# The two output projections of a two-layer encoder, computed as seven products of sums of blocks instead of eight products of blocks

## The chip, the cores and the metric

The kernel runs on one core of a Trainium2 chip. The metric is the device time of one execution in microseconds (us). All inputs and outputs are float32, and the weights, tables and activations lie in DRAM at the start.

## The reference, cut to what matters

```python
def reference(x, mem, ...):                 # x: (1, 1024, 1024), mem: (1, 256, 1024)
    memn = rmsnorm(mem, mem_norm_gain)
    for l in range(2):
        h = rmsnorm(x, norm_gain[l])
        ...
        if l == 0:   # 8 global heads, 8 window heads of 64; 4 memory heads of 128
            ya, yb, ym = global_gqa(...), window_gqa(...), memory_attn(...)
            y = jnp.concatenate([ya, yb, ym], axis=-1) * jax.nn.silu(gate)
            x = x + y @ w_out_even[e]       # (1024 x 1536) @ (1536 x 1024)
        else:        # 16 neighbourhood heads of 64; 4 memory heads of 128
            yc, ym = neighborhood_attn(...), memory_attn(...)
            y = jnp.concatenate([yc, ym], axis=-1) * jax.nn.silu(gate)
            x = x + y @ w_out_odd[o]        # (1024 x 1536) @ (1536 x 1024)
    return rmsnorm(x, final_norm_gain)
```

The change concerns the two lines with `w_out`, the output projections. Each maps 1536 rows of gated attention outputs (12 tiles of 128 rows) to 1024 columns (8 tiles of 128), for 1024 tokens (two halves of 512).

## The kernel before, in words

**Layout.** Activations lie transposed: 128 features on the partitions, tokens along the free dimension. A float32 matmul is done as three matmuls in the format F32R: each operand is split into a high part (a rounded copy, `copy`, L88 on ACT) and a low part (operand minus high part), and TensorE adds high×high, high×low and low×high in PSUM. One such matmul has 512 tokens as its moving side.

**What stands ahead of an output projection.** In layer 0 the heads come in the order global pairs 0 to 3, memory heads, window pairs 0 to 3; in layer 1 the memory heads come first and then eight neighbourhood pairs. Behind each pair or memory head, `gated` (L308) projects the gate with SiLU (`gate`, L295), multiplies the head's output by it (L314 or L320), and stores the product in a DRAM tile `yd[k]`, one of 12. In layer 0 the product is stored as it is; in layer 1 it is split here, and high and low parts are stored (ACT L88, DVE L322). A window pair goes in chunks: scores (L476, L477), sums with bias on DVE (L479), exponentials on ACT, scaling with the softmax denominators on POOL (L500), transposes (L96), a split of the transposed probabilities (`p_parts`, ACT L88 and DVE L332) and the product with the values (L515). A neighbourhood pair has the same steps at L875/L876, L883, L887, L889, L96, L88/L332 and L858.

**The output projection** (`out_project`, L917). For each half of the tokens it goes over the 8 column tiles two at a time, and for these over the 12 row tiles in units of four, the unit of the memory heads first (order 2, 0, 1). For the first half and the first four column tiles that unit's matmuls are issued ahead of the others, and can stand between the matmuls of the last attention pair. `project` (L123) loads the weights of each unit and column tile (128 x 512, `wload`), splits them (`wparts`, L112: high part on POOL L118; low part L119 on DVE in layer 0 and on POOL in layer 1), and issues 12 matmuls of 512 tokens (L134). So one layer has 8 x 12 x 3 x 2 = 576 matmuls; in layer 1 the last column tile of the second half goes in two quarters of 256 tokens (L985). `y_parts` (L900) loads the gated outputs back from DRAM; in layer 0 it splits them there (ACT L88, DVE L92), through a buffer `ph`. The sink of a column tile adds the residual to the PSUM result (L940, DVE), squares it (L941, ACT) and adds the squares up (L951, POOL). `done` then makes the norm: `rstd_cols` (L204, tiny matmuls), `rows_of` (transposes, L96) and, for layer 0, `norm_split` (L217 to L219), or, behind layer 1, the scaling by norm and gain (L1100 on POOL, L1102 on DVE) and the stores of the output (L1103).

**What sets the order.** The order of the instructions of each engine is fixed when the kernel is built: a scheduler orders them by a simulated timeline and by priorities (`ahead`, with the table `AHEAD`, L29). Each engine runs its instructions in that order, and SP issues nearly all the transfers, in one queue. PSUM has 8 banks of 512 columns. SBUF tiles come from pools by tag; a new tile with a tag waits until the oldest one of that tag has been read for the last time. Tag `H` has 16 tiles, which hold the normed input of a layer (8 tiles, high and low).

## Time and profile before

| what | us |
|---|---|
| three timed runs | 1612.15, 1610.36, 1612.3 (median 1612.15) |
| the profiled execution, its own time | 1608.82 |
| the span of its trace | 1607.0 |

The profiled execution's own time and the span of its trace differ by 1.82 us, which lie before the first and after the last traced instruction. Its mean granted TensorE clock is 0.989 of full speed.

How to read the profile: PE is TensorE (matmuls), PEld its loads of stationary operands, DVE is VectorE, ACT ScalarE, POOL GpSimd, SP the queue that issues transfers. A group of instructions is told as its line, engine and operation, output<-inputs by the program's names, shapes, count, busy time and mean duration in ns, then the idle time of the engine just before them and what ended most of it. A row of a timeline is start, length, engine, line, operation, tiles, count, and in brackets the wait ahead of it and what ended that wait. A row of the view of windows gives for a stretch its length, then for each engine its busy time and its number of instructions, the granted clock of TensorE, the share of the DMA engines' time in use, and GB/s. The chain of waits goes back from the last instruction, at each step to what released it.

In the profiled execution, layer 0's output projection lies between about 680 us (where its first matmuls stand between those of the last window pair) and 849 us, and layer 1's between about 1441 us and 1595 us, near the end of the span.

### The profile page before, as it was taken

The numbers are of one execution on the slowest core, as the hardware profiler recorded it, in microseconds if no ns is written. First come the engines' busy times: TensorE is split into PE (matmuls) and PEld (weight loads), VectorE is DVE, ScalarE is ACT, GpSimd is POOL, SyncE is SP. The second block draws the span as 40 slices with busy tenths as digits, with TensorE's granted clock in tenths as the row PEclk, the third lists the DMA queues.
The fourth block names the chain that finished last, engine by engine and source line by source line (L and its number), as shares of the span: only waits on it lengthen the run. The fifth ranks groups of instructions, "written<-read, shape, count | busy, mean of one in ns | idle before, by whom it ended". The sixth has DMA issues, their size and how long they took to land.

```text
span 1607.0 us, 24242 instructions
## 1 busy us (share of the span) xinstructions
PE 1551.9 (97%) x8394; PEld 1323.8 (82%) x8394; DVE 957.5 (60%) x2124; ACT 706.6 (44%) x1626; POOL 655.3 (41%) x801
## 2 busy tenths in 40 slices
PE   6999999999999999989999999999999999999997
PEld 6899888888887888867788888888888888888886
DVE  7768577766667678864764444655555555554122
ACT  8633564655446355641313333534544445443110
POOL 2522232332323133224454335544444444445885
PEclk7999999999999999999999999999999999999998
DMA  9524111025211111135552324213222222235772
GB/s 352 180 97 152 66 40 53 29 50 83 75 66 27 67 62 50 50 117 185 182 171 87 104 87 125 83 66 91 64 76 83 66 79 79 71 107 177 238 260 79
DMA packets 97858, 167.88 MB, mean 104 GB/s; under 512 B 9504, under 2 KB 30240, under 8 KB 97736
## 3 DMA queue, kind: packets, MB, share of 16 engines
q1 hardware_dynamic: 96760, 165.51, 32.4%
q8 instruction: 66, 1.08, 0.3%
q10 hardware_dynamic: 976, 0.82, 0.2%
q14 instruction: 56, 0.46, 0.1%
HBM read 120.17 MB, written 36.70 MB: 98 GB/s over the span
## 4 chain that ended last, share of the span: by engine, by line
PE 85%; DVE 7%; ACT 3%; DMA 3%; issue 2%; POOL 0%; SPq 0%; DVEq 0%; ACTq 0%; POOLq 0%
PE pj L163 42%; PE sa L134 8%; PE tr L96 7%; PE pj L134 5%; PE s L134 3%; PE pv L816 3%; PE pj L617 2%; PE pv L858 2%; DVE pl L332 2%; PE s L875 1%; PE s L876 1%; PE sa L787 1%; PE pv L515 1%; PE sa L788 1%; DVE st L792 1%
## 5 line engine op out<-in xcount | busy, mean ns | idle before, releaser
L163 PE MATMUL pj<-H,wh 128*128 128x512 f32 x1952 | 628.3, 397 | 1.7 <-ACT bt L941 1.5
L163 PEld LDWEIGHTS pj<-H,wh 128*128 128x128 f32 x1952 | 358.8, 188 | 71.4 <-POOL wh L118 1.9
L163 PE MATMUL pj<-H,wl 128*128 128x512 f32 x976 | 386.3, 396 | 0.0
L118 POOL TENSOR_SCALAR wh<-wraw 128x512 fp32r<-128x512 f32 x226 | 151.4, 672 | 396.4 <-PE pj L163 252.0
L88 ACT ACTIVATE ph<-tr 128x512 fp32r<-128x512 f32 (+2 forms) x336 | 177.9, 540 | 243.9 <-PE tr L96 232.4
L332 DVE TENSOR_TENSOR pl<-tr,ph 128x512 fp32r<-128x512 f32 (+2 forms) x336 | 205.0, 615 | 101.9 <-ACT ph L88 98.9
L163 PEld LDWEIGHTS pj<-H,wl 128*128 128x128 f32 x976 | 183.6, 188 | 37.4
L119 POOL TENSOR_TENSOR wl<-wraw,wh 128x512 fp32r<-128x512 f32 x136 | 180.0, 1329 | 23.3 <-ACT wh L88 13.4
L795 POOL TENSOR_SCALAR P<-P,st 128x1024 f32<-128x1024 f32 x64 | 76.0, 1188 | 171.7 <-DVE st L794 162.0
L119 DVE TENSOR_TENSOR wl<-wraw,wh 128x512 fp32r<-128x512 f32 x116 | 90.3, 789 | 63.4 <-POOL wh L118 61.7
L96 PE MATMUL tr<-ident,P 128*128 128x128 f32 x816 | 123.0, 273 | 2.4 <-DVE pl L332 2.2
L889 POOL TENSOR_SCALAR pn<-pn,st 128x384 f32<-128x384 f32 (+1 forms) x128 | 71.6, 567 | 100.3 <-DVE st L888 99.4
L96 PEld LDWEIGHTS tr<-ident,P 128*128 128x128 f32 x816 | 95.7, 140 | 14.0 <-PE sa L788 7.1
L887 ACT ACTIVATE pn<-pn,st 128x384 f32<-128x384 f32 (+1 forms) x128 | 74.4, 583 | 47.3 <-DVE st L886 46.6
L792 DVE TENSOR_REDUCE st<-sa 128x1 f32<-128x1024 f32 x64 | 77.6, 1217 | 15.8 <-PE sa L788 13.5
L793 ACT ACTIVATE P<-sa,st 128x1024 f32<-128x1024 f32 x64 | 71.5, 1117 | 32.3 <-PE tr L96 14.5
L883 DVE CUSTOM_DVE_ANT_0 pn<-s,bm 128x384 f32<-128x384 f32 x96 | 51.4, 554 | 43.5 <-PE s L876 39.9
L816 PE MATMUL pv<-pl,va 128*128 128x256 f32 x256 | 69.5, 297 | 6.3 <-DVE pl L332 6.1
L617 PE MATMUL pj<-ah,H 128*128 128x256 f32 x384 | 73.1, 286 | 0.0
L235 DVE TENSOR_TENSOR vt<-pj,rows 128x512 f32<-128x512 f32 x60 | 41.2, 686 | 53.4 <-PE pj L163 53.4
L88 ACT ACTIVATE bt<-pv 64x512 f32<-64x512 f32 (+1 forms) x80 | 40.8, 510 | 71.8 <-PE pv L816 25.9
L816 PE MATMUL pv<-ph,va 128*128 128x256 f32 x256 | 72.1, 298 | 0.0
(323 smaller groups left out, 3142.6 us busy)
## 6 DMA issues: line engine op xcount, KB each, us to landing
wraw<-w_o SPq DMA_DIRECT2D x80, 256.0 KB, 2.6
wraw<-w_oe SPq DMA_DIRECT2D x48, 256.0 KB, 3.0
wraw<-w_oo SPq DMA_DIRECT2D x48, 256.0 KB, 3.1
wraw<-w_e SPq DMA_DIRECT2D x44, 256.0 KB, 2.5
k<-k SPq DMA_DIRECT2D x36, 256.0 KB, 3.7
wraw<-w_mem SPq DMA_DIRECT2D x32, 256.0 KB, 4.3
y<-yb SPq DMA_DIRECT2D x12, 512.0 KB, 2.7
y<-sg SPq DMA_DIRECT2D x24, 256.0 KB, 2.4
```

What stands on the lines that cost most here:

```text
L88: return self.nc.scalar.activation(out, in_, AF.Copy, scale=scale)
L96: self.nc.tensor.transpose(o, i, self.ident)
L118: nc.gpsimd.tensor_scalar(hf, raw, 1.0, 1.0, op0=OP.mult, op1=OP.mult)
L119: (nc.gpsimd if self.wsplit[1] == "pool" else nc.vector).tensor_tensor(lf, raw, hf, op=OP.subtract)
L134: self.last = nc.tensor.matmul(a[:, :n], s[:, k, :], moving(u * UNIT + k, c, n)[m], start=(u == units[0] and k == 0 and i == 0), stop=(u = ...
L163: last = nc.tensor.matmul(a[:, :n], s[:, kt % UNIT, :], m, start=(kt == 0 and i == 0), stop=(kt == KT - 1 and i == 2))
L332: nc.vector.tensor_tensor(pl[:, :n], tr[:, :n], ph[:, :n], op=OP.subtract)
L617: self.last = nc.tensor.matmul(a[:, b * 256:(b + 1) * 256], x[kt][:, t], w, start=(kt + b + i == 0), stop=(kt == KT - 1 and i == 2), skip_ ...
L792: nc.vector.tensor_reduce(st[:, 0:1], s, axis=AX.X, op=OP.max, negate=True)
L795: nc.gpsimd.tensor_scalar(pt, pt, st[:, 2:3], 0.5, op0=OP.mult, op1=OP.mult)
L816: nc.tensor.matmul(o[:, :256], v[:, c + k, kv, :], part[:, k * 256:(k + 1) * 256], start=(c + k == 0 and part is parts[0]), stop=(c + k == ...
L887: nc.scalar.activation(o, o, AF.Exp, bias=st[:, 1:2], accum_out=st[:, 2:3])
```

## The change

The 8 column tiles, the 12 row tiles and the 1024 tokens are each halved. With the weights as four blocks (a11 and a12: columns 0 to 3 with the first and the second half of the rows; a21 and a22: columns 4 to 7 with the same) Winograd's form of Strassen's scheme computes the four result blocks from seven products. The row tiles are renumbered by `ROWS`, in the weights too (on the host, as part of the layout): the first half holds the memory heads 0 to 3 and the pairs 0 and 1, the second half the pairs 2 to 7. In the program's order the products are

1. a11 x y(first half of rows, second tokens), to banks x, and to the result c11 (columns 0 to 3, second tokens)
2. s1 = a21 + a22, x t1 = y(first rows, first tokens) - y(first rows, second tokens), to banks y, and to c22 (columns 4 to 7, first tokens)
3. s2 = s1 - a11, x t2 = y22 - t1, added to banks x; to c12 (columns 0 to 3, first tokens). Here y22 is the second rows' first tokens
4. s3 = a11 - a21, x t3 = y22 - y(first rows, first tokens), added to banks x; to c22 and c21 (columns 4 to 7, second tokens)
5. s4 = a12 - s2, x y22, added to banks y; to c12. The first token half is done, and its norm runs beside product 6
6. a12 x y21 (second rows, second tokens), to banks x; c11 is done
7. a22 x t4 = t2 - y21, its result subtracted from c21

Each product has 4 column tiles x 6 row tiles x 3 = 72 matmuls of 512 tokens: 504 a layer instead of 576. The last column tile of product 7 in layer 1 goes in two quarters of 256 tokens, of 18 matmuls each instead of 36. A weight unit is now 128 x 384 (three row tiles, 9 matmuls), and 56 of them come up per layer instead of 48 of 128 x 512. Their high part is copied on ACT; their low part (L962) is taken on DVE, or for a11, a12 and a22 on DVE and POOL by turns (`either`). The blocks a11 and s1 are kept in tiles of tag `H`.

`gated` now stores, for the six heads or pairs of the first half, four pieces of 512 tokens: high and low part of the second tokens, the difference first minus second tokens (a subtraction on POOL), and the first tokens; for the other six it stores the product as it is, in both layers.

```diff
+ROWS = (8, 9, 10, 11, 0, 1, 2, 3, 4, 5, 6, 7)
...
-    def gated(self, w, nt, y, dst, parts=False):
+    def gated(self, w, nt, y, dst):
...
+        with self.ahead("gate"):
+            nc.vector.tensor_tensor(y, y, sg, op=OP.mult)
+            if len(dst.shape) == 2:
                 nc.sync.dma_start(dst, y)
+                return
+            nc.gpsimd.tensor_tensor(sg[:, first], y[:, first], y[:, second], op=OP.subtract)
+            h, l = sg.bitcast(F32R)[:, second], y.bitcast(F32R)[:, second]
+            self.copy(h, y[:, second])
+            nc.vector.tensor_tensor(l, y[:, second], h, op=OP.subtract)
+            for i, t in enumerate((sg[:, second], y[:, second], sg[:, first], y[:, first])):
+                nc.sync.dma_start(dst[:, i, :], t)
...
+    def y_parts(self, yd, tags, kind, t=None, y22=None):
...
+                if kind == "y11":
+                    load(tile.bitcast(F32), y0[:, 0:2, :])
+                    continue
+                if kind == "t1":
+                    load(t[k], y0[:, 2, :])
+                    raw = t[k]
+                elif kind == "t2":
+                    load(y22[k], y1[:, first])
+                    minus(t[k], y22[k], t[k])
+                    raw = t[k]
...
+                self.copy(hi, raw)
+                (nc.gpsimd if kind == "t1" else nc.vector).tensor_tensor(lo, raw, hi, op=OP.subtract)
...
+    def w_parts(self, raw, engine):
+        h, l = (self.st(t, [128, UNIT, 128], F32R, pool=self.base, bufs=4)[:, :3] for t in ("wh", "wl"))
...
+        self.copy(hf, raw)
+        engine.tensor_tensor(lf, raw, hf, op=OP.subtract)
...
     def out_project(...):
...
+                    elif kind == "s1":
+                        raw = ws[i][:, c]
+                        nc.gpsimd.tensor_tensor(raw, raw, load(a(4 + i, 0)[:, c]), op=OP.add)
+                    elif kind == "s2":
+                        raw = ws[i][:, c]
+                        nc.vector.tensor_tensor(raw, raw, wa[i][:, c], op=OP.subtract)
...
+                    yield self.w_parts(raw, self.either() if kind[0] == "a" else nc.vector)
...
+        def residual(x, nt, half):
+            nc.sync.dma_start(x, res[nt][:, 512 * (2 - half):512 * (3 - half)])
+        def plus(x, p, op=OP.add):
+            nc.vector.tensor_tensor(x, x, p, op=op)
...
+        for i in range(4):
+            product(y, xb[i], weights(i, "s2"), False)
+            residual(at(c12, i), i, 2)
+            with self.ahead("sink"):
+                plus(at(c12, i), xb[i])
```

In the changed file the lines are six or more further on: L500 is there L506, L515 is L521, L889 is L895, and L134's matmuls stand at L1018.

**What moves.** The first place is POOL at the last window pair of layer 0. P tiles are the probabilities of a chunk of that pair (L500 and L506 scale them), wh and wl a weight unit's high and low part, mk, sg, q and k in the changed kernel tiles of t1 and its parts, and H a tile of s1. Before:

```order
L500 TENSOR_SCALAR P_7586<-P_7586,st_7583 128x384 x2
L500 TENSOR_SCALAR P_7594<-P_7594,st_7583 128x384 x2
L118 TENSOR_SCALAR wh_7978<-wraw_7976 128x512
L500 TENSOR_SCALAR P_7660<-P_7660,st_7657 128x384 x2
L500 TENSOR_SCALAR P_7668<-P_7668,st_7657 128x384 x2
L500 TENSOR_SCALAR P_7734<-P_7734,st_7731 128x384 x2
L500 TENSOR_SCALAR P_7742<-P_7742,st_7731 128x256 x2
L118 TENSOR_SCALAR wh_8008<-wraw_8006 128x512
L118 TENSOR_SCALAR wh_8014<-wraw_8012 128x512
L118 TENSOR_SCALAR wh_8044<-wraw_8042 128x512
```

In the changed kernel:

```order
L506 TENSOR_SCALAR P_7696<-P_7696,st_7693 128x384 x2
L506 TENSOR_SCALAR P_7704<-P_7704,st_7693 128x384 x2
L931 TENSOR_TENSOR mk_8056<-H_8226,mk_8056 128x512
L962 TENSOR_TENSOR wl_8012<-H_7996,wh_8011 128x384
L955 TENSOR_TENSOR q_8060<-mk_8056,q_8060 128x512
L1003 TENSOR_TENSOR H_8154<-H_8154,wraw_8156 128x384
L955 TENSOR_TENSOR k_8061<-sg_8057,k_8061 128x512
L1003 TENSOR_TENSOR H_8154<-H_8154,wraw_8172 128x384
L955 TENSOR_TENSOR k_8062<-sg_8057,k_8062 128x512
L1003 TENSOR_TENSOR H_8190<-H_8190,wraw_8192 128x384
L1003 TENSOR_TENSOR H_8190<-H_8190,wraw_8208 128x384
L931 TENSOR_TENSOR mk_8056<-H_8226,mk_8056 128x512
```

There the scaling of the pair's last chunk (P_7770; before it is P_7734) comes behind these rows and the next two:

```order
L962 TENSOR_TENSOR wl_8042<-H_8026,wh_8041 128x384
L931 TENSOR_TENSOR sg_8057<-H_8227,sg_8057 128x512
L506 TENSOR_SCALAR P_7770<-P_7770,st_7767 128x384 x2
L506 TENSOR_SCALAR P_7778<-P_7778,st_7767 128x256 x2
L931 TENSOR_TENSOR sg_8057<-H_8227,sg_8057 128x512
```

Before, POOL's scalings of the last two chunks follow one upon the other with no other work between them; in the changed kernel twelve subtractions and additions of the output projection stand between P_7704 and P_7770.

The second place is PE at the end of the same pair (`pv` is its product with the values, `tr` a transpose or, in the changed kernel, also a bank of banks x or y). Before:

```order
L515 MATMUL pv_7732<-pl_7781,v_5851 128x2x128
L515 MATMUL pv_7732<-ph_7780,v_5851 128x2x128
L515 MATMUL pv_7732<-pl_7781,v_5851 128x2x128
L515 MATMUL pv_7732<-ph_7791,v_5851 128x2x128
L515 MATMUL pv_7732<-pl_7792,v_5851 128x2x128
L134 MATMUL sa_7932<-k_7892,wh_8008 128x512 x2
L134 MATMUL sa_7932<-k_7892,wl_8009 128x512
```

In the changed kernel:

```order
L521 MATMUL pv_7768<-ph_7803,v_5881 128x2x128
L521 MATMUL pv_7768<-pl_7804,v_5881 128x2x128
L521 MATMUL pv_7768<-ph_7816,v_5881 128x2x128
L1018 MATMUL tr_7925<-q_7911,wh_8028 128x512 x2
L1018 MATMUL tr_7925<-q_7911,wl_8029 128x512
L1018 MATMUL tr_7925<-q_7912,wh_8028 128x512 x2
L1018 MATMUL tr_7925<-q_7912,wl_8029 128x512
L1018 MATMUL tr_7925<-k_7913,wh_8028 128x512 x2
```

Before, the values of the last chunk are followed by matmuls on the rows of unit 0; in the changed kernel the last column tile of product 1 stands inside them, and its other three column tiles (54 matmuls) stand ahead of the last chunk's transposes.

The third place is POOL at the last neighbourhood pair of layer 1 (`pn` are the probabilities of a block of 128 queries). Before:

```order
L889 TENSOR_SCALAR pn_15230<-pn_15230,st_15231 128x256
L119 TENSOR_TENSOR wl_15575<-wraw_15572,wh_15574 128x512
L889 TENSOR_SCALAR pn_15240<-pn_15240,st_15241 128x384
L889 TENSOR_SCALAR pn_15259<-pn_15259,st_15260 128x384
L889 TENSOR_SCALAR pn_15279<-pn_15279,st_15280 128x384
L889 TENSOR_SCALAR pn_15299<-pn_15299,st_15300 128x384
L889 TENSOR_SCALAR pn_15321<-pn_15321,st_15322 128x384
L889 TENSOR_SCALAR pn_15346<-pn_15346,st_15347 128x384
L118 TENSOR_SCALAR wh_15604<-wraw_15602 128x512
```

In the changed kernel:

```order
L895 TENSOR_SCALAR pn_15229<-pn_15229,st_15230 128x256
L955 TENSOR_TENSOR k_15640<-H_15636,k_15640 128x512
L962 TENSOR_TENSOR wl_15591<-H_15575,wh_15590 128x384
L955 TENSOR_TENSOR q_15642<-H_15637,q_15642 128x512
L1003 TENSOR_TENSOR H_15662<-H_15662,wraw_15664 128x384
L1003 TENSOR_TENSOR H_15662<-H_15662,wraw_15680 128x384
L1003 TENSOR_TENSOR H_15698<-H_15698,wraw_15700 128x384
L1003 TENSOR_TENSOR H_15698<-H_15698,wraw_15716 128x384
L895 TENSOR_SCALAR pn_15263<-pn_15263,st_15264 128x256
L895 TENSOR_SCALAR pn_15273<-pn_15273,st_15274 128x384
L931 TENSOR_TENSOR H_15637<-mk_15807,H_15637 128x512
L962 TENSOR_TENSOR wl_15621<-H_15605,wh_15620 128x384
```

Before, the scalings of the last blocks stand with few weight splits (L118, L119) between them; in the changed kernel the parts of t1 and the sums s1 stand in groups of up to six between two scalings.

300 lines of the change are left out of this document (185 added, 115 removed).

## The prediction

> **What bounds the kernel now.** I read the page first, then the chain of waits, then windows around the two projections, then the timelines of single engines there.
>
> On the page, the first rows are the span and the busy times, and the row of shares is the chain that ended last, by engine:
>
> ```profile
> span 1607.0 us, 24242 instructions
> PE 1551.9 (97%) x8394; PEld 1323.8 (82%) x8394; DVE 957.5 (60%) x2124; ACT 706.6 (44%) x1626; POOL 655.3 (41%) x801
> PE 85%; DVE 7%; ACT 3%; DMA 3%; issue 2%; POOL 0%; SPq 0%; DVEq 0%; ACTq 0%; POOLq 0%
> ```
>
> TensorE is the bound: busy for 97% of the span. Whatever takes matmuls away gains their full time, as long as nothing else becomes late. The chain in order of time has, in the two projections, these pieces (start, length, what):
>
> ```profile
> 713.28 3.25 DMA ph<-y
> ...
> 1481.29 4.73 DMA mk<-y
> ...
> 1544.00 16.48 PE s L134 x72
> 1560.48 16.48 PE pj L134 x72
> ```
>
> The last two give the price of a matmul of 512 tokens: 16.48/72 = 0.2289 us from start to start. The first two are transfers of gated outputs back from DRAM, that TensorE waits for. The windows show how much it waits:
>
> ```profile
> core 0: us, PE busy (x) PEld busy (x) DVE busy (x) ACT busy (x) POOL busy (x), PEclk, DMA share, GB/s
> 680.00:849.00 169.00, 158.67 (x725) 128.20 (x724) 102.10 (x169) 48.46 (x96) 71.70 (x80) 0.99 0.50 159
> 688.00:709.00 21.00, 19.22 (x111) 16.19 (x110) 13.42 (x35) 9.56 (x27) 7.43 (x13) 1.00 0.20 64
> 709.00:725.00 16.00, 10.15 (x43) 7.22 (x40) 8.23 (x15) 6.29 (x11) 0.00 (x0) 0.89 0.66 213
> 725.00:849.00 124.00, 121.29 (x530) 97.86 (x531) 74.41 (x103) 27.63 (x45) 61.07 (x62) 1.00 0.55 176
> 1441.00:1481.00 40.00, 40.00 (x218) 34.60 (x217) 20.21 (x70) 16.85 (x44) 20.96 (x27) 1.00 0.46 150
> 1481.00:1486.00 5.00, 3.42 (x16) 2.28 (x14) 1.38 (x2) 1.10 (x2) 3.61 (x4) 1.00 0.82 233
> 1540.00:1560.00 20.00, 20.00 (x89) 16.43 (x88) 5.27 (x8) 1.90 (x3) 19.92 (x24) 1.00 0.69 225
> ```
>
> In layer 0's projection (680 to 849) TensorE is idle for 169.00 - 158.67 = 10.3 us: 1.8 in 688 to 709, beside the last window pair's chain, 5.9 in 709 to 725, where that pair's output goes to DRAM and back, and 2.7 behind it. In layer 1's it is idle for 5.00 - 3.42 = 1.6 us, and full in 1441 to 1481. Between 709 and 725 the granted clock is 0.89, and the timeline of TensorE shows why:
>
> ```profile
> 717.39 1.43 PE L134 MATMUL sa<-k,wh 128*128 128x512 f32 x2 [3.24 <-ACT k L88]
> 718.61 0.63 PE L134 MATMUL sa<-k,wl 128*128 128x512 f32 x1
> ...
> 721.12 0.40 PE L134 MATMUL sa<-k,wl 128*128 128x512 f32 x1
> ```
>
> Behind the wait, eight matmuls start between 717.39 and 721.12: 3.73 us instead of 8 x 0.2289 = 1.83. A long wait costs 1.9 us more behind it.
>
> **Matmuls that go.** 576 - 504 = 72 per layer, 144 in all, and all stand on the path: 144 x 0.2289 = **-33.0 us**.
>
> **Stalls that go.** Products 1 and 2 need the first six row tiles alone, whose heads are long done; the last pairs are first asked for in product 3, 144 matmuls or 33.0 us into the projection, and the round trip through DRAM took less than the 16 us of its window. So 10.3 + 1.9 (layer 0) and 1.6 (layer 1) go: **-13.8 us**. (The 2.7 behind 725 I count with it, since the order of that part is replaced as a whole.) If the first two products were delayed by something else, part of this cover would go as well; that is the next part.
>
> **What is added on DVE and POOL.** Per layer DVE gets 68 subtractions of two SBUF operands at 128x384 (weights: 44 low parts, 24 sums) and 30 at 128x512 (parts of t1 to y21), besides 32 sums with PSUM in place of 16; POOL gets 20 of 128x384 and 36 of 128x512 (18 differences, 6 low parts, 12 sums of squares), and no more copies of weights. The prices, in the timelines of POOL and DVE:
>
> ```profile
> 743.70 0.91 POOL L118 TENSOR_SCALAR wh<-wraw 128x512 fp32r<-128x512 f32 x1 [0.31 <-PE sa L134]
> 781.42 1.53 POOL L951 TENSOR_TENSOR vt<-vt,bt 128x512 f32<-128x512 f32 x1 [3.89 <-ACT bt L941]
> 842.24 2.54 POOL L119 TENSOR_TENSOR wl<-wraw,wh 128x512 fp32r<-128x512 f32 x2
> 1596.35 1.41 POOL L1100 TENSOR_TENSOR sg<-sg,vt 128x256 f32<-128x256 f32 x2 [8.13 <-ACT vt L88]
> ```
>
> ```profile
> 743.43 0.69 DVE L119 TENSOR_TENSOR wl<-wraw,wh 128x512 fp32r<-128x512 f32 x1 [2.81 <-POOL wh L118]
> 744.04 1.28 DVE L940 TENSOR_TENSOR yb<-sa,pl 128x512 f32<-128x512 f32 x2
> 745.24 0.68 DVE L119 TENSOR_TENSOR wl<-wraw,wh 128x512 fp32r<-128x512 f32 x1
> 781.72 1.78 DVE L119 TENSOR_TENSOR wl<-wraw,wh 128x512 fp32r<-128x512 f32 x1
> 1594.87 0.42 DVE L940 TENSOR_TENSOR yb<-pj,pl 128x256 f32<-128x256 f32 x1
> ```
>
> POOL: 2.54/2 = 1.27 for 512 columns, 1.41/2 = 0.70 for 256, so 0.98 for 384. DVE: 743.43 to 745.24 holds three of 512 columns, 0.60 each; 0.42 for 256, so 0.50 for 384. Beside each other they are dearer: at 781.72 DVE's subtraction took 1.78 in place of 0.69 and ended at 783.50, 0.55 behind POOL's end at 782.95; POOL's copy at 743.70, beside a subtraction of DVE, took 0.91. DVE's sums at 744.04, whose one operand is in PSUM, ran beside that same copy at their usual length. So subtractions of SBUF operands take turns with POOL. Their sum per layer is 68 x 0.50 + 30 x 0.60 = 52 us on DVE and 20 x 0.98 + 36 x 1.27 = 65 us on POOL, 117 us together, against 504 x 0.2289 = 115.4 us of matmuls. Neither engine is over its time alone; in strict turns the two just fill the projection, so each piece that comes late is late by a turn, and the order's slack (units of weights ahead, four buffers) is what hides it. POOL was busy for 19.92 us of 20.00 in 1540 to 1560, with 5.27 on DVE beside it and TensorE full, so such a load can be carried. I price lateness in layer 0 at 4 us (0 to 8), in layer 1 at 2 (0 to 4).
>
> The Trainium skill, "SBUF — State Buffer", section "SBUF: two separate sides", says that the pair of ports which the two engines share is "an exclusive lock, not a bandwidth split", held for a whole instruction by whichever of a DVE operation with two SBUF inputs and a GpSimd operation started first. The rows above agree (1.78 in place of 0.69). Without such a lock the 4 and the 2 would fall away, and the sum would be 6 us lower.
>
> **New waits at the start of layer 0's projection.** In the timelines of POOL (first row), TensorE and DVE, in the chain, in the page's groups and in its transfers stand the prices of what follows the last gate projection:
>
> ```profile
> 696.81 4.32 POOL L500 TENSOR_SCALAR P<-P,st 128x384 f32<-128x384 f32 x8 [8.50 <-DVE st L495]
> ```
>
> ```profile
> 687.12 0.39 PE L163 MATMUL pj<-H,wl 128*128 128x512 f32 x1
> ```
>
> ```profile
> 715.75 1.23 DVE L314 TENSOR_TENSOR yb<-yb,sg 128x1024 f32<-128x1024 f32 x1
> ```
>
> ```profile
> 630.23 0.59 PE pv L515 x5
> 631.53 0.44 PE tr L96 x4
> ```
>
> ```profile
> L88 ACT ACTIVATE ph<-tr 128x512 fp32r<-128x512 f32 (+2 forms) x336 | 177.9, 540 | 243.9 <-PE tr L96 232.4
> ...
> wraw<-w_oe SPq DMA_DIRECT2D x48, 256.0 KB, 3.0
> ```
>
> The last window pair's last two chunks were scaled one behind the other, in the eight operations of the first row. By the order, twelve operations of POOL now stand between the two chunks: six of 512 and six of 384 columns, 6 x 1.27 + 6 x 0.98 = 13.5 us. The first chunk's four are through at 696.81 + 4 x 4.32/8 = 699.0, so the last one's first two are done at 699.0 + 13.5 + 1.1 = 713.6 without turns lost to DVE, and at 717.6 if DVE takes 8 turns of 0.50; I take 716. TensorE has, from 688 (the last gate projection's last matmul starts at 687.12), 54 matmuls of product 1 (12.4 us) and of the pair 30 values at 0.59/5 = 0.118, 24 transposes at 0.44/4 = 0.11 and 8 scores of 384 columns, by their width 0.17 each: 7.5 us. It stands at 707.9, so it waits **8.1 us** (5.7 to 9.7), and 1.9 more at half speed behind it. Then product 2's last two row tiles lie in a tile of tag `sg` that comes free only with the gating of this pair: copy 0.54, subtraction 0.7, gating 1.23, transfer 3.0, the new tile's high part 0.54 and two operations on POOL 2.54, with 0.6 for the issues 9.2 us behind the last values, in which TensorE has 33 matmuls, 7.6 us: **1.6 us** (0 to 4). With 4 for turns, layer 0 gets 8.1 + 1.9 + 1.6 + 4 = **+15.6 us**.
>
> **New waits in layer 1's projection.** The first matmuls of the projection used to follow the last gate projection's at once, as the timeline of TensorE, the chain and the page's group of scalings show:
>
> ```profile
> 1444.19 0.39 PE L163 MATMUL pj<-H,wl 128*128 128x512 f32 x1
> ```
>
> ```profile
> 1441.83 1.85 PE pj L163 x8
> ```
>
> ```profile
> L889 POOL TENSOR_SCALAR pn<-pn,st 128x384 f32<-128x384 f32 (+1 forms) x128 | 71.6, 567 | 100.3 <-DVE st L888 99.4
> ```
>
> Now a11 goes into a tile of tag `H`, free only when that gate projection has read it, at about 1442.3, in the piece of eight matmuls; load 3.0 and split 1.0 give 1446.3 instead of 1444.4: **2 us** (1 to 3). Among the last pair's last 13 scalings (0.567 each, 7.4 us) stand by the order 19 operations for t1, s1 and low parts, 7 of 512 and 12 of 384 columns: 20.6 us. From 1446 POOL is through them at 1474, with 4 to 6 us of turns at 1478 to 1480; the transposes and values behind the last one end near 1484, where TensorE's window ended full at 1481: **3 us** (0 to 8). With 2 for turns: **+7.0 us**.
>
> **The end.** Behind the last matmul stand the last quarter's norm, scaling and stores; in the timeline of DVE the first quarter's scalings are
>
> ```profile
> 1597.16 1.65 DVE L1102 SCALAR_TENSOR_TENSOR yb<-yb,gain,tr 128x256 f32<-128x256 f32 x4
> ```
>
> The quarters have 18 matmuls in place of 36 (a quarter's matmul has half the columns), so the second is through 18 x 0.2289/2 = 2 us sooner behind the first, while the first one's scalings (1.65 on DVE, 1.41 on POOL) are still queued: **+1.4 us** (0 to 2). In `gated` the first six heads get more work in layer 0 (1.27 on POOL, 0.54 on ACT, 0.60 on DVE each), and in layer 1 the last six less; TensorE, 97% busy, covers it, the last pairs have none of it, and uncovered it would be 2.4 us for each of six heads, 14 in all, which I leave to the slower rival. Loads of weights are cut in smaller transfers, of nearly the same bytes; at a DMA share of 0.50 to 0.69 I price them at nothing (0 to 3).
>
> **Sum.** -33.0 - 13.8 + 15.6 + 7.0 + 1.4 = **-22.8 us**. The profiled execution (1608.82, 3.3 below the median) would come to 1586.0; from the median, 1612.15 - 22.8 = 1589.4.
>
> **Rivals.**
> - *The gain is nearly full.* The scheduler's order holds, POOL's twelve operations run without lost turns and TensorE's own waits cover each other; 5 us of new waits are left: -33.0 - 13.8 + 5 + 1.4 = -40.4, **1572 us**. For it: TensorE full beside a full POOL in 1540 to 1560. Against it: the twelve operations are in the order, and there is no other work for TensorE behind the 54 matmuls. 0.12.
> - *All new waits at their upper ends.* Layer 0 9.7 + 1.9 + 4 + 8 = 23.6, layer 1 3 + 8 + 4 = 15, end 2: -6.2, **1606 us**. For it: waits add up where the same two engines serve them all. 0.15.
> - *Slower: the turns decide.* If DVE and POOL fill only 80% of their common time, because each waits for ACT's copies and loads in between, layer 0's work after 688 (117 us, 12 us of the norm, 4 of scalings: 133) takes 166 us and ends at 854 in place of 849, and layer 1's (117, 7 of scalings, 4 of the norm: 128, from 1441) takes 160 and ends at 1601 in place of 1595: with the end's 1.4 that is +12, **1624 us**. It decides from a filling of 0.83 (133/161) downwards. For it: 781.72. Against it: DVE's sums with PSUM run free, and 25.2 us of both engines' work fit in 20 us in 1540 to 1560. The Trainium skill's rule quoted above is the one by which this would be so. 0.12.
> - *No change*, waits that eat it all between the last two: 0.04. That the matmuls are not fewer is excluded by the order, which has 504 per layer.
>
> My forecast has the remaining 0.57, with 1580 to 1600 as its own range. What a measurement here can tell from no change is about 0.2%, 3.2 us. Faster: 0.57 + 0.12 + 0.14 = 0.83; within 0.2%: 0.05; slower: 0.12. The range goes from all new waits at their lower ends (7.6 in layer 0, 1 in layer 1: -46.8 + 8.6 = -38, 1574) to just past the second rival, 1608; it leaves out the slower rival and part of the fullest gain.
>
> **What would show it.** Right: in the profile after, 504 matmuls per projection at 0.23 us; no wait for `y` from the last pairs; a wait of 6 to 10 us of TensorE around 708 to 716 for the transposes of the last chunk, released by POOL's L506; a short wait at 1444; DVE's L962 and POOL's rows longer than alone. Wrong: waits spread over products 3 to 7, released by DVE or POOL (the third rival), or hardly any wait at 708 (the first), or a wait for loads of weights.

## The result, and the profile after

The changed kernel took 1646.88 us (median of 4 runs, 1646.03 to 1651.77), the kernel before 1611.26 us: ratio 1.0228, 95% interval 1.0205 to 1.0250. So it is 35.6 us slower, where 22.8 us faster was forecast. The page of the profiled execution:

```profile
span 1644.4 us, 24244 instructions
PE 1539.8 (94%) x8232; PEld 1309.3 (80%) x8232; DVE 1054.6 (64%) x2256; ACT 777.7 (47%) x1774; POOL 656.3 (40%) x757
PE 75%; DVE 9%; DMA 6%; issue 4%; ACT 3%; POOL 2%; SPq 0%; DVEq 0%; ACTq 0%; POOLq 0%
```

TensorE is busy for less time than before, in a longer span, and the chain that ended last lies more on DVE (9% for 7%), DMA (6% for 3%) and POOL. To see where, I set marks on TensorE's timeline: the last matmul of each layer's last gate projection, and the last matmul of each output projection. After the change:

```profile
723.25 0.39 PE L170 MATMUL pj<-H,wl 128*128 128x512 f32 x1
884.02 0.39 PE L1018 MATMUL tr<-va,wl 128*128 128x512 f32 x1
1482.53 0.40 PE L170 MATMUL pj<-H,wl 128*128 128x512 f32 x1
1631.19 0.28 PE L1018 MATMUL pj<-v,wl 128*128 128x256 f32 x1
```

Before, the gates' marks are the rows of 687.12 and 1444.19 above, and the projections end with

```profile
846.99 0.39 PE L134 MATMUL sa<-P,wl 128*128 128x512 f32 x1
...
1594.56 0.28 PE L985 MATMUL pj<-mk,wl 128*128 128x256 f32 x1
```

| stretch, us | before | after | change |
|---|---|---|---|
| up to layer 0's last gate projection | 687.1 | 723.3 | +36.1 |
| layer 0's output projection | 159.9 | 160.8 | +0.9 |
| layer 1 up to its last gate projection | 597.2 | 598.5 | +1.3 |
| layer 1's output projection | 150.4 | 148.7 | -1.7 |
| from there to the end of the span | 12.4 | 13.2 | +0.8 |
| span | 1607.0 | 1644.4 | +37.4 |

Two things stand out. The whole loss lies ahead of the first changed product. And the two projections, with 72 matmuls (16.5 us) less each and without the old stalls, are as long as they were.

**Ahead of the projections.** The windows of the changed kernel show TensorE, and every other compute engine, at rest around 390 us, with the granted clock at half:

```profile
core 0: us, PE busy (x) PEld busy (x) DVE busy (x) ACT busy (x) POOL busy (x), PEclk, DMA share, GB/s
380.00:390.00 10.00, 0.03 (x1) 0.00 (x0) 0.00 (x0) 0.00 (x0) 0.00 (x0) 0.62 0.52 75
390.00:400.00 10.00, 0.00 (x0) 0.00 (x0) 0.00 (x0) 0.00 (x0) 0.00 (x0) 0.50 0.50 62
```

The waits of TensorE in that stretch have one row (in total, times, longest), and the timeline of ACT names what ACT waited for:

```profile
PE pv L822 <- ACT ph L95: 27.5, 1, 27.5
```

```profile
405.28 0.63 ACT L309 ACTIVATE sg<-vt 128x512 f32<-128x512 f32 x1 [31.82 <-DMA y<-sg]
```

ACT's next instruction is a gate (L309), which writes a tile `sg`; that tile can't be written before its old content has been stored. Behind it in ACT's queue stands the copy `ph` that TensorE needs. The queue of transfers at that time, and the view of the DMA queues (KB each, median us from issue to landing):

```profile
357.61 0.32 SPq L330 DMA_DIRECT2D y<-yb  x1
357.98 0.85 SPq L452 DMA_DIRECT2D band_rows<-bias  x1
359.90 13.58 SPq L107 DMA_DIRECT2D wraw<-w_e  x1
373.58 9.27 SPq L330 DMA_DIRECT2D y<-sg  x2
382.94 4.61 SPq L330 DMA_DIRECT2D y<-yb  x1
```

```profile
band_rows<-bias SPq DMA_DIRECT2D x1, 2048.0 KB
y<-sg SPq DMA_DIRECT2D x2, 256.0 KB, 28.9
```

Between the pieces of pair 1's output stands the store of the window heads' bias rows, 2 MB out of 8 partitions. Between 380 and 400 us the DMA engines move 62 to 75 GB/s at half their share, single issues behind it take 5 to 14 us, and the two pieces in `sg` need 28.9 us to land. The kernel before has the same store at the same place:

```profile
351.25 0.32 SPq L315 DMA_DIRECT2D y<-yb  x1
351.62 0.86 SPq L446 DMA_DIRECT2D band_rows<-bias  x1
...
397.85 0.38 SPq L315 DMA_DIRECT2D y<-yb  x1
```

But there pair 1's one store stands ahead of it, and `sg` is never stored: it is free as soon as the output has been multiplied by it.

**In the projections.** The windows there, of the changed kernel, with the columns as above:

```profile
723.00:757.00 34.00, 26.02 (x135) 21.15 (x133) 30.98 (x54) 18.21 (x45) 31.59 (x31) 0.90 0.69 247
757.00:783.00 26.00, 23.40 (x102) 18.22 (x102) 18.05 (x28) 11.05 (x22) 9.23 (x7) 1.00 0.55 160
783.00:820.00 37.00, 36.72 (x160) 30.11 (x161) 32.32 (x53) 16.18 (x31) 7.69 (x5) 1.00 0.32 98
820.00:860.00 40.00, 33.07 (x124) 25.72 (x123) 30.81 (x46) 18.28 (x34) 22.24 (x16) 0.83 0.57 183
860.00:884.00 24.00, 22.26 (x97) 17.66 (x96) 22.02 (x26) 12.55 (x23) 15.43 (x13) 0.99 0.41 122
1482.00:1520.00 38.00, 33.01 (x168) 27.12 (x167) 29.38 (x81) 23.26 (x59) 31.70 (x33) 0.94 0.69 248
1545.00:1600.00 55.00, 50.49 (x212) 39.86 (x211) 49.29 (x72) 27.85 (x53) 24.79 (x18) 0.97 0.38 121
```

TensorE's idle time is spread: 8.0 us beside the last window pair, 2.6, 0.3, 6.9 and 1.7 us behind it, and 9.5 us in the two stretches of layer 1; in the stretches with 5 to 8 us of it the granted clock is 0.83 to 0.94. DVE, in its third pair of numbers, is busy for 69 to 92% of these stretches, and for 83% of the five of layer 0 together. The longest waits of TensorE in 723 to 884 us:

```profile
PE pv L521 <- DVE yb L531: 6.8, 3, 5.7
PE tr L1018 <- DVE wl L962: 3.5, 1, 3.5
PE pv L1018 <- DVE wl L962: 2.2, 1, 2.2
PE pj L1018 <- DVE wl L962: 2.0, 1, 2.0
```

The longest wait of the first row, 5.7 us, lies in the last window pair, at its last chunk but one; the other rows are low parts of weights that DVE has late. The chunk too waits for DVE, and not for POOL's scaling (L506): its products with the values go into a PSUM bank that DVE has to empty first of the chunk before (L531), and that stands behind subtractions for the projection's weights. The timelines of DVE and, with the scaling of the last chunk, of POOL:

```profile
745.74 2.88 DVE L1000 TENSOR_TENSOR wraw<-H,wraw 128x384 f32<-128x384 f32 x2
748.54 1.37 DVE L1006 TENSOR_TENSOR H<-H,H 128x384 f32<-128x384 f32 x1
749.83 0.83 DVE L531 TENSOR_TENSOR yb<-pv,bt 64x256 f32<-64x256 f32 x2
```

```profile
751.02 2.73 POOL L506 TENSOR_SCALAR P<-P,st 128x384 f32<-128x384 f32 x4
```

TensorE goes on at 750.81, before that scaling has begun. Why DVE is late shows in its timeline further on, beside POOL's:

```profile
829.03 0.55 DVE L962 TENSOR_TENSOR wl<-wraw,wh 128x384 fp32r<-128x384 f32 x1
829.50 1.64 DVE L1009 TENSOR_TENSOR wraw<-wraw,H 128x384 f32<-128x384 f32 x1
831.07 0.55 DVE L962 TENSOR_TENSOR wl<-wraw,wh 128x384 fp32r<-128x384 f32 x1
```

```profile
829.31 1.41 POOL L1034 TENSOR_TENSOR vt<-vt,bt 128x512 f32<-128x512 f32 x1 [3.96 <-ACT bt L1032]
```

A subtraction of two SBUF tiles of this size takes 0.55 us alone and 1.64 us beside POOL's sum, which began 0.19 us earlier and ends at 830.72; DVE ends 0.42 us later. This is the exclusive lock of the Trainium skill's "SBUF — State Buffer", section "SBUF: two separate sides", and the row agrees with it.

### The profile page after: what moved, and what is told of

It is laid out like the page before. It is cut to its first block, busy times and chain, and to the rows that moved or that the text cites. A ratio compares the mean times of both kernels' runs of the same rounds, so it can differ in the third digit from the quotient of the medians.

```text
span 1644.4 us, 24244 instructions
## 1 busy us (share of the span) xinstructions
PE 1539.8 (94%) x8232; PEld 1309.3 (80%) x8232; DVE 1054.6 (64%) x2256; ACT 777.7 (47%) x1774; POOL 656.3 (40%) x757
## 4 chain that ended last, share of the span: by engine, by line
PE 75%; DVE 9%; DMA 6%; issue 4%; ACT 3%; POOL 2%; SPq 0%; DVEq 0%; ACTq 0%; POOLq 0%
PE pj L170 39%; PE tr L103 7%; PE pj L1018 3%; PE pv L822 3%; PE pv L864 2%; PE pj L623 2%; PE tr L1018 2%; DMA y<-sg 2%; PE pj L141 2%; DVE pl L338 2%; PE sa L793 1%; PE sa L794 1%; PE s L881 1%; PE pv L521 1%; PE sa L1018 1%
## 5 line engine op out<-in xcount | busy, mean ns | idle before, releaser
L125 POOL TENSOR_SCALAR wh<-wraw 128x512 fp32r<-128x512 f32 x130 | 84.3, 649 | 241.8 <-PE pj L170 188.6
L126 POOL TENSOR_TENSOR wl<-wraw,wh 128x512 fp32r<-128x512 f32 x88 | 116.0, 1320 | 23.0 <-ACT wh L95 14.5
L895 POOL TENSOR_SCALAR pn<-pn,st 128x384 f32<-128x384 f32 (+1 forms) x128 | 72.9, 577 | 108.3 <-DVE st L894 104.3
L822 PE MATMUL pv<-ph,va 128*128 128x256 f32 x256 | 72.2, 299 | 27.5 <-ACT ph L95 27.5
L889 DVE CUSTOM_DVE_ANT_0 pn<-s,bm 128x384 f32<-128x384 f32 x96 | 51.4, 554 | 44.1 <-PE s L882 36.3
L126 DVE TENSOR_TENSOR wl<-wraw,wh 128x512 fp32r<-128x512 f32 x68 | 52.7, 780 | 32.2 <-POOL wh L125 29.6
```

The costliest lines, as they stand in the source:

```text
L125: nc.gpsimd.tensor_scalar(hf, raw, 1.0, 1.0, op0=OP.mult, op1=OP.mult)
L126: (nc.gpsimd if self.wsplit[1] == "pool" else nc.vector).tensor_tensor(lf, raw, hf, op=OP.subtract)
L822: nc.tensor.matmul(o[:, :256], v[:, c + k, kv, :], part[:, k * 256:(k + 1) * 256], start=(c + k == 0 and part is parts[0]), stop=(c + k == ...
```

## The experiments

All ran beside the kernel before; each has 4 to 10 runs. The last three columns are stretches of the profiled execution, between the marks above: from the first matmul of `tokens` (L163 or its counterpart, at 171.5 to 174.8 us in all of them) to layer 0's last gate projection, and the two output projections. They can be compared as long as the same work stands on the same side of a mark: in the first stretch that is 2889 matmuls in every kernel but sg_three (2893), diff_early and prep_held (2833 each).

| kernel | median us | ratio to before, interval | heads of layer 0 | projection 0 | projection 1 |
|---|---|---|---|---|---|
| before | 1611 | 1 | 515.6 | 159.9 | 150.4 |
| changed | 1646.88 | 1.0228, 1.0205 to 1.0250 | 549.0 | 160.8 | 148.7 |
| band_act | 1639.57 | 1.0173, 1.0156 to 1.0190 | 541.4 | 159.1 | 151.8 |
| band_early | 1649.16 | 1.0232, 1.0212 to 1.0252 | 550.4 | 165.7 | 152.7 |
| sg_three | 1652.81 | 1.0247, 1.0232 to 1.0262 | 560.8 | 155.7 | 152.3 |
| band_late | 1625.67 | 1.0093, 1.0065 to 1.0122 | 525.0 | 161.5 | 151.7 |
| chunk_first | 1641.52 | 1.0181, 1.0163 to 1.0198 | 541.6 | 162.5 | 151.3 |
| low_dve | 1646.07 | 1.0208, 1.0188 to 1.0227 | 543.3 | 161.5 | 155.6 |
| low_turns | 1646.78 | 1.0205, 1.0188 to 1.0222 | 541.7 | 161.8 | 160.7 |
| no_weight_sums | 1625.70 | 1.0086, 1.0058 to 1.0113 | 541.5 | 165.6 | 141.4 |
| no_differences | 1612.16 | 0.9997, 0.9983 to 1.0011 | 541.3 | 147.8 | 136.9 |
| late_no_differences | 1594.79 | 0.9901, 0.9882 to 0.9921 | 524.8 | 144.5 | 138.2 |
| diff_early | 1624.82 | 1.0082, 1.0069 to 1.0094 | 524.6 | 168.1 | 147.7 |
| prep_held | 1622.01 | 1.0065, 1.0050 to 1.0080 | 524.6 | 165.4 | 148.6 |

### The stall ahead of the projections: band_act, band_early, sg_three, band_late

**band_act**

```diff
-        self.tc.keep_in_program_order(nc.sync.dma_start(band, mk[:, None, :].to_broadcast([8, 128, 512])))
+        nc.scalar.dma_start(band, mk[:, None, :].to_broadcast([8, 128, 512]))
```

> The changed kernel with one edit: the 2 MB store of the bias rows (band_rows<-bias) is issued by ACT's queue instead of SP's. Theory: 30 us of the loss lie ahead of the projections, where TensorE stands still from 380 to 407 us: the stores of pair 1's pieces stand behind that 45 us store in SP's queue, they hold the tile sg, and the next gate waits for it. Then the time falls by the 27.5 us of the wait and 2 to 3 us at half clock, to about 1617 us. Rival: it is the number and size of the new stores themselves (four of 256 KB a head in place of one of 512 KB); then the stall stays and the time is above 1640 us.

1639.57 us: neither, and near the rival's 1640. The wait shrank, but the gate still stood for its tile, as ACT's timeline shows:

```profile
390.80 0.63 ACT L309 ACTIVATE sg<-vt 128x512 f32<-128x512 f32 x1 [18.53 <-DMA y<-sg]
```

TensorE waited 14.2 us for it in place of 27.5. Another queue does not take the store out of the way: the loads of the bias rows, which need it landed, were issued at 397.9 us, and the two pieces in `sg`, issued from 361.3 us on, took 24 us to land. The Trainium skill, "DMA: Bandwidth & Descriptors", section "Queues, rings and completion order", says that SP's and ACT's queues have their rings on the same 16 DMA engines, which take turns between them; the 18.53 us agree.

**band_early**

```diff
-            if j == 1:
+            if j == 0:
                 band = self.band_rows()
```

> The changed kernel with the bias rows made one pair earlier (behind pair 0 in place of pair 1), the store still in SP's queue. Theory: the store then runs from about 285 us, and the next gate that needs a tile sg comes at about 345 us, more than the 45 us of the store later, so the stall vanishes too: about 1617 us. Rival: whatever stands behind that store in SP's queue stalls TensorE wherever it is placed (weights too): above 1640 us.

1649.16 us: the theory failed. The order put the store between the pieces of pair 0 in the same way (its first piece at 262.98, the bias rows at 263.35, the pieces in `sg` at 278.99 us), and TensorE waited for 27.5 us again, there. My reckoning of when the next gate comes was wrong: not at 345 us, but next in ACT's queue from 278.8 us on (it ran at 310.63, behind a wait of 31.83 us for `y<-sg`). The time is as the rival had it, but what TensorE waited for is again the tile, and band_late below shows that the place does matter.

**sg_three**

```diff
-... P=6, ph=3, pl=3, sg=2, yb=2, ...
+... P=5, ph=3, pl=3, sg=3, yb=2, ...
-            c=(("P", "P"), ("P", "P"), ("P", "P"), ("yb", "yb"))),
+            c=(("P", "P"), ("P", "P"), ("P", "sg"), ("yb", "yb"))),
```

> The changed kernel with three tiles of tag sg in layer 0 in place of two (and five of tag P in place of six; one result tile of the projection moves from P to sg). The store of the bias rows stays in SP's queue. Theory: what stalls TensorE at 380 us is not the transfers but the tile sg, which the next gate writes and which is held until the pair's pieces have landed; with a third tile the wait of 27.5 us and what follows it at half clock go, and so do the waits of 2 to 3 us behind the earlier heads: 1612 to 1618 us. Rival: the stores and loads stuck behind the bias rows are themselves what TensorE waits for: above 1635 us.

1652.81 us: the expectation failed. The row of waits shows a new long one in place of the old:

```profile
PE pv L822 <- DVE yb L828: 27.7, 11, 21.3
```

21.3 us, now for the output tile `yb` (two of them), whose last piece stood behind the bias rows too: it was issued at 388.61 us and landed 24.1 us later, at 412.7, and the sum that writes the next `yb` (L828) starts at 412.82. The trace names no releaser there, but the times leave little else. So neither side of the expectation is right as it stands: a third `sg` moves the stall to the next tile that a late store holds. The other ten waits of this row, 6.4 us, and those for `pl` I put down to the tile P that is missing: the edit seems to cost something of its own, and so its total is no measure of the stall.

**band_late**

```diff
-            if j == 1:
+            if j == 2:
                 band = self.band_rows()
```

> The changed kernel with the bias rows made one pair later (behind pair 2), the store in SP's queue. Three tiles of sg did not end the stall, since then the output tile yb was what the next head waited for: what is held is every tile whose pieces stand behind the bias rows' store while the next head is near. Behind pair 2 there is one store of its output ahead of the bias rows and none of its own behind it, and the next head that wants a tile held by memory head 2's pieces comes about 80 us later. Theory: no wait above 4 us ahead of the projections, 30 us below the changed kernel: about 1614 to 1620 us. Rival: memory head 2's four stores, which now stand behind the bias rows, stall the next head in the same way: above 1635 us.

1625.67 us, 21 us below the changed kernel, where 27 to 33 were expected. The long wait is gone; in the whole of the heads of layer 0 the largest rows of waits are

```profile
PE pv L822 <- DVE pl L338: 6.5, 12, 0.9
PE pj L170 <- DVE vt L242: 5.4, 2, 2.7
```

and the stretch is 525.0 us, 24.0 shorter. Pair 2 is in the second half, and its one store stands ahead of the bias rows. What is left, 9.4 us over before, holds 6.1 us more of TensorE's idle time (18.3 for 12.2), most of it the second row, which before doesn't have (2 x 2.7 us). As I read it, a gate waits for its tile there although the pieces land in 2.5 us; the trace names DVE and not the transfer. The rest of the 9.4 I did not take apart. The two projections, in another order, are 3.7 us longer than the changed kernel's; the two profiled executions differ by 22.5 us in all.

### What makes the projections long: chunk_first, low_dve, low_turns, no_weight_sums, no_differences

**chunk_first** (`late` is a wait in the order, behind the last scaling of the last window pair)

```diff
+    def late(self):
+        return self.tc.issue_after(self.scaled.ins) if self.scaled else nullcontext()
...
+                with self.late():
+                    nc.gpsimd.tensor_tensor(o, x, y, op=OP.subtract)
...
+                        with self.late():
+                            nc.gpsimd.tensor_tensor(raw, raw, low, op=OP.add)
```

> As band_act, and in layer 0's projection POOL's twelve additions and subtractions for t1 and s1 are held back until the last chunk of the last window pair is scaled. Theory of the prediction: the wait of TensorE at 745 to 751 us (5.75 us, and about 2 at half clock) goes: 7 to 8 us below band_act. Rival (the two engines' turns decide): the same work only comes later, product 2 waits for it, and the time stays within 2 us of band_act.

1641.52 us, no faster than band_act, as the rival had it. The wait did go (0.5 us is left for L531), so POOL's twelve operations, or the order that comes with them, were behind it, though it was DVE that came late. But others came, as the rows of waits in its projection of layer 0 show:

```profile
PE sa L1026 <- DVE wl L965: 7.3, 5, 4.4
PE tr L1026 <- DVE wl L965: 3.1, 2, 2.9
PE pv L521 <- ACT ph L95: 1.9, 2, 1.0
```

Low parts of weights are late by 10.4 us in these two rows alone, in place of 8.1 in all in band_act, and the projection is 3.4 us longer; TensorE is idle in it for 21.1 us, in band_act for 21.2. The queue ahead of the last chunk is where the lateness first shows, and not its cause.

**low_dve** and **low_turns**

```diff
-                    yield self.w_parts(raw, self.either() if kind[0] == "a" else nc.vector)
+                    yield self.w_parts(raw, nc.vector)           # low_dve
+                    yield self.w_parts(raw, self.either())       # low_turns
```

> As band_act, with all low parts of the projections' weights on DVE, none on POOL. If DVE and POOL only take turns, what counts is their common work, which falls by 12 x (0.98 - 0.50) = 5.8 us per layer: 3 to 8 us below band_act. If DVE's own queue is what is late (80 to 90% busy in the projections), its 6 us more per layer are paid: 3 to 10 us above band_act.

> As band_act, with all low parts of the projections' weights by turns on DVE and POOL (28 and 28 per layer in place of 44 and 12). If turns are the bound, the common work rises by 16 x 0.48 = 7.7 us per layer: 3 to 12 us above band_act. If DVE's queue alone is late, it is relieved of 8 us per layer: 3 to 12 us below.

1646.07 and 1646.78 us, both about 7 us above band_act, at the edge of the noise (by the ratios to before, 5 to 6 us; the intervals just touch). low_turns came out as turns would have it; low_dve, with less common work, came out as a late DVE would have it. So, if these differences are real, neither "only the sum counts" nor "only DVE counts" holds: DVE's own load and the turns bind together, and the split of the changed kernel is the best of the three.

**no_weight_sums** (three lines left out)

```diff
-                        nc.vector.tensor_tensor(raw, wa[i][:, c], raw, op=OP.subtract)
-                        nc.vector.tensor_tensor(raw, raw, wa[i][:, c], op=OP.subtract)
-                        nc.vector.tensor_tensor(raw, raw, ws[i][:, c], op=OP.subtract)
```

> As band_act, without DVE's 24 differences of weights per layer (s2, s3 and s4 are left out, their inputs used in their place; all loads and splits stay): 12 us less of DVE's work per layer. By either theory that is the bound's own work, so 8 to 20 us below band_act; if the transfers of weights are what is late, within 3 us of it.

1625.70 us, 14 us below band_act, as expected of either theory, so that it does not choose between them. Layer 1's projection is 10.4 us shorter. The profiled execution was the slowest of its runs (1632.57), with a wait of 7.0 us of a tiny norm matmul for POOL's sum of squares in layer 0, so that its 165.6 us there say little of the median.

**no_differences**

```diff
-            minus = lambda o, x, y: nc.gpsimd.tensor_tensor(o, x, y, op=OP.subtract)
+            minus = lambda o, x, y: None
...
-                        nc.gpsimd.tensor_tensor(raw, raw, load(a(4 + i, 0)[:, c]), op=OP.add)
+                        load(a(4 + i, 0)[:, c])
```

> As band_act, without POOL's 26 sums and differences per layer (t1 to t4 and s1 are left out, their inputs used in their place; all loads and splits stay). Turns of DVE and POOL as the bound: their common work falls by 18 x 1.27 + 8 x 0.98 = 30.7 us per layer, most waits of the projections go, and the time is 25 to 40 us below band_act, about 1600 to 1615 us. If DVE's own queue is late, whatever POOL does: less than 8 us below band_act.

1612.16 us, 27.4 us below band_act: as turns have it. Not one of DVE's operations was taken away, and yet DVE is through sooner. Two of its groups, low parts and differences of weights, in the projection of layer 0, first of the changed kernel and then of this one (busy time, mean ns of one):

```profile
L962 DVE TENSOR_TENSOR wl<-H,wh 128x384 fp32r<-128x384 f32 x19 | 15.2, 798 | 5.8 <-ACT wh L95 5.8
L1006 DVE TENSOR_TENSOR H<-H,H 128x384 f32<-128x384 f32 x8 | 7.2, 903 | 0.2
```

```profile
L960 DVE TENSOR_TENSOR wl<-H,wh 128x384 fp32r<-128x384 f32 x19 | 11.8, 626 | 3.6 <-ACT wh L95 3.6
L1004 DVE TENSOR_TENSOR H<-H,H 128x384 f32<-128x384 f32 x8 | 4.9, 608 | 0.2
```

The windows of layer 0's projection, of band_act and of this kernel, and that of layer 1's of this kernel:

```profile
714.00:874.00 160.00, 138.85 (x617) 111.61 (x616) 135.38 (x204) 76.64 (x152) 88.01 (x71) 0.96 0.52 166
713.00:861.00 148.00, 136.59 (x615) 110.50 (x613) 115.68 (x202) 75.94 (x151) 49.14 (x45) 0.97 0.52 165
1458.00:1596.00 138.00, 135.33 (x649) 112.42 (x647) 101.73 (x207) 73.36 (x154) 49.70 (x49) 0.99 0.47 158
```

DVE is busy for 19.7 us less in layer 0 on nearly the same number of operations, and TensorE for 92% of that window, in layer 1 for 98%. The sums left out were also links that copies and low parts had to wait for; how much of the gain is that, no run separates. 61 us less of POOL's work in the two layers give 27 us of time.

### Both causes at once, and two tries to keep the computation

**late_no_differences** has the edits of band_late and no_differences.

> As band_late, without POOL's 26 sums and differences per layer (their inputs used in their place). If the stall ahead of the projections and the common work of DVE and POOL are the two causes and add, 27 us below band_late, as no_differences was below band_act: 1587 to 1594 us, the time that the prediction gave. If they share a cause, well above 1600 us.

1594.79 us, 30.9 below band_late, where no_differences was 27.4 below band_act: the two causes add, within 3.5 us. It is 0.99 of the kernel before (0.9882 to 0.9921). It comes within 6 us of the time that the prediction gave for the whole change, but without sums that the prediction had counted in, so it does not bear the forecast out.

**diff_early** moves 18 differences of a layer to where the heads are made:

```diff
+            if row >= 6:
+                nc.sync.dma_start(dst[:, 0:2, :].rearrange("p a b -> p (a b)"), y)
+                nc.sync.dma_start(sg[:, first], yd[row - 6][:, 2, :])
+                nc.sync.dma_start(sg[:, second], yd[row - 6][:, 3, :])
...
+                minus(sg[:, first], y[:, first], sg[:, first])
+                minus(t4, sg[:, first], y[:, second])
+                minus(sg[:, second], y[:, first], sg[:, second])
```

> As band_late, with the 18 differences t2, t3 and t4 of each layer (all but POOL's 8 sums s1) moved out of the projection: gated makes them for each of the second half's heads, on POOL, when that head is done (it loads two pieces of the first half's head back into the free tile sg, and stores three more pieces), and the projection only loads and splits them. All of the computation is kept. If DVE's and POOL's common work inside the projections is the bound, it falls by 18 x 1.27 = 23 us per layer out of the 30.7 that no_differences left out; three quarters of its 27 to 31 us are 20 to 23 us, of which the longer gating may take back up to 8: 1603 to 1614 us, at or just below the kernel before. If lateness of DVE alone or of transfers were the bound: within 5 us of band_late, above 1620 us.

1624.82 us: the expectation failed, and the time is the one it gave for late transfers or a late DVE. By the marks the heads of layer 0 cost nothing more (524.6 us), layer 1's projection gained 4.0 us, and layer 0's is 6.6 us longer than in band_late. But the mark stands elsewhere in the work here: 56 matmuls of the last window pair, about 7 us of TensorE by the prices of the prediction (an estimate), lie behind it instead of ahead of it. By this estimate it is the heads, with their longer gating, that became about 7 us longer (TensorE's idle time in them is 3.5 us more), and layer 0's projection, without these matmuls, stayed about as long. TensorE's idle time in it fell from 22.7 to 18.6 us. Most of that is beside the last window pair:

```profile
700.00:730.00 30.00, 23.89 (x120) 18.86 (x118) 23.24 (x59) 16.11 (x43) 22.98 (x27) 0.89 0.45 141
730.00:760.00 30.00, 20.73 (x102) 17.07 (x100) 16.15 (x32) 13.67 (x29) 7.13 (x7) 0.83 0.65 203
```

TensorE is idle for 15.4 of 60 us and at a granted clock of 0.89 and 0.83. From 760 us to the end of the projection it is idle for 3.3 us, where band_late has 10.7 from 760 on: there the moved differences do help. Behind 730 neither DVE nor POOL is busy for long: there the chain of waits has ACT at a copy for product 2 that waits 6.0 us for its load (731.92 to 737.95), and the pair's copies stand behind it.

**prep_held** is diff_early with `late` around the parts of t1 and t2, the sums s1 and s2 and their parts, in both layers.

> As diff_early, and what prepares product 2 and 3 (parts of t1 and t2, sums s1 and s2 and their parts, on POOL, DVE and ACT) is held back in both layers until the last attention pair's last probabilities are scaled. diff_early took 4 us from layer 1's projection, but layer 0's became 6.6 us longer: there TensorE was idle for 15.4 of 60 us beside the last window pair's last chunks, whose steps are queued behind this preparation. Theory: with it out of their way those waits fall by about 10 us in layer 0 and 4 in layer 1, and the gain of the moved differences shows: 1608 to 1614 us, about the kernel before. Rival: the preparation is then late itself and product 2 waits for it, as in chunk_first: within 3 us of diff_early's 1625 us.

1622.01 us: the rival's case, 2.8 us below diff_early. Its mark stands as in diff_early. So no kernel that keeps the computation was faster than the one before; the best, prep_held, is at 1.0065 (1.0050 to 1.0080).

## Why the prediction was wrong, point by point

- **Matmuls that go, -33.0.** Right: matmuls of 512 tokens still start 0.23 us apart (three of them from 883.33 to 884.02 us), and late_no_differences, where little else is late, has projections of 144.5 and 138.2 us for 159.9 and 150.4, though it leaves sums out.
- **Stalls that go, -13.8.** Right in the main: of TensorE's waits in layer 0's projection 0.4 us are for a part made of a gated output (ACT's copy for product 2), where before it was 10.3 us with its surroundings.
- **"In `gated` the first six heads get more work ... TensorE, 97% busy, covers it", nothing, or 14 uncovered.** This is the step that failed. It counted the instructions and not what they hold: the new stores read `sg` and keep it, so that a gate two heads later depends on their landing, and one of them stood behind 2 MB that the kernel before sent out unnoticed. It cost 36.1 us by the mark: 29.9 of it between the multiplications of two heads that bracket the stall (365.19 to 452.13 us before, 371.59 to 488.45 after), 6.4 ahead of it, of which 2.8 lie ahead of layer 0's first projection, where the executions differ by 3 us among themselves. The bias rows' store was there to be read in the timeline of SP before, with 18.60 us for two issues behind it, and the prediction looked at that queue only around the projections.
- **New waits of layer 0's projection, +15.6.** By the marks 0.9 + 16.5 + 12.2 = 29.6, of which TensorE's idle time between the marks is 19.5. A wait was there at the forecast place, 5.7 us (5.7 to 9.7 forecast), but its path was another: the last chunk's transposes were to wait for POOL's scaling (L506), and it was the chunk before whose products with the values waited for DVE (L531). That the size came out at the edge of the range is in part luck. The 1.6 for product 2's last row tiles came out as 0.4. The term for turns was mis-sized: 4 forecast (0 to 8), and the waits behind 757 us make 11.5 us of idle time, 8.9 of it for low parts of weights, with the low clock besides. And the wait of 5.7 us was no term of its own: taken away in chunk_first it came back elsewhere.
- **New waits of layer 1's projection, +7.0.** By the marks -1.7 + 16.5 + 1.6 = 16.4; idle time is 10.0 of it. The 2 us for a11 at the start did not come: the first matmul of the projection starts at 1482.76, 0.23 behind the mark. What came is spread over the projection, as in layer 0.
- **The end, +1.4.** 0.8.
- **The rivals.** The slower one named the mechanism that fits the projections best. Its 1624 us needed 57 us of new waits there (12.4 + 46.8 - 1.4 at the end), and 29.6 + 16.4 = 46.0 came, which alone is no change (-46.8 + 46.0 + 0.8). The loss stood in no case at all. band_late's 1625.67 us are near that rival's time by accident: 9.4 us of it still lie ahead of the projections.
- **The sum.** Of the 60.2 us between forecast and profiled execution 36.1 are the heads of layer 0 and 23.4 the two projections.

What stays open is how the waits of the projections divide between turns, POOL's sums as links that the parts wait for, and loads that are late because the four buffers of weights come free late: no_differences takes the first two away together, and diff_early, which only moves 18 of the 26, gained far less. Open are also the 4 us of the 9.4 in band_late that its long waits do not hold.

## What to carry to other kernels

Count for every new store which tile it holds, who writes that tile next, and what stands ahead of it in its queue: a transfer that nobody waited for may be 45 us long. When matmuls are traded for sums on DVE and POOL, add up their two-operand SBUF work as one resource against TensorE's new, shorter time (here 117 us against 115.4), and expect waits when the two are near each other. And a wait that is removed by order alone, while that resource is full, can come back behind it, as in chunk_first. When two kernels are compared between marks, count the work on each side of the mark first.

## What the runs showed of the hardware that I had not expected

A 2 MB store from 8 partitions took about 45 us (its readers' loads were issued 45.3 us behind it), and single issues behind it in its queue took 5 to 14 us; on ACT's queue it still slowed SP's stores (18.53 us of waiting). POOL's work, at 26 operations less per layer, was worth 0.45 us of time per us of its own (27.4 of 61.4), without any operation of DVE being removed.
